# Sixty instructions change places within their engine's queue in a hybrid attention layer

## The chip, the cores and the metric

The kernel runs on one core of a Trainium2 chip. The core has five engines with a queue of instructions each: TensorE (PE, matrix products; its weight loads are listed apart as PEld), VectorE (DVE), ScalarE (ACT), GpSimd (POOL) and SyncE (SP), which in this kernel issues every DMA. [...] The metric is the time of one execution on the device in microseconds (us), lower is better. A profiled execution is a little different from the timed ones, so its own time is given beside its span.

## The reference

One layer of an encoder: a norm, one input projection, two kinds of attention side by side, an output projection and an embedding gate. It is computed for a prompt of 1024 tokens and a sample of 32 tokens that has caches of 512 positions.

```python
qa, ka, va, ga, qb, kb, vb, gb = split(rmsnorm(h, g_pre) @ w_in)   # 8 x 512 columns
oa = band_attention(qa, ka, va)       # 8 heads of 64, own 64-frame chunk and the 8 before, relative bias, softmax
ob = stick_breaking(qb, kb, vb)       # 8 heads of 64, strictly causal
# stick-breaking: w = exp(log_sigmoid(z) + sum over later keys of log_sigmoid(-z))
y  = concat([oa * silu(ga), ob * silu(gb)]) @ w_out
h  = h + rmsnorm(y, g_post)
h  = h + sigmoid(h @ w_ple_gate) * (p @ w_ple)
return h for prompt and sample, and the new keys and values of both
```

All of it is float32. D_MODEL is 1024, w_in is 1024 x 4096, and the keys and values that are returned are those of each of the 16 heads.

## The kernel before

**Tiling and stages.** The 1056 tokens are worked in three groups of 352 columns. Products are made in a reduced float32 form, and each operand is split into a high and a low part (names with h and l: `wh_`, `wl_`, `wTh`, `wTl`), so that most products are three matmuls. The attention goes in eight stages, one pair of heads each, in turn A (band) and B (stick-breaking): A0, B0, A1, B1 and so on to A3 and B3. In a stage the two heads' scores, weights and values are woven with the projection (`col_steps`) of a later pair's q, k or v. Names carry this: `wTlA31_1` is the low part of the turned weights of A, pair 3, head 1, second set; `wr_vB3_0` the first half of the raw weight columns of v for pair 3 of B. After the stages follow the gates (`mm_g...`), then the output projection and the embedding gate.

**What the stages move by DMA.** The steps that the change and the prediction speak of:

- `load_w` (line 689) loads raw weight columns `wr_...`, two halves of 256 KB. `ensure` (line 701) has them rounded on ACT or POOL (`wh_`) and the rest subtracted on POOL (`wl_`).
- `weights_t` (line 1107) turns the attention weights. A part goes through PE (`ptw`, then ACT `wTh`, DVE `wTl`). The rest goes over a DRAM scratch: a transposed tile `om` is stored to `swap...`, four loads bring it back into `wTl`, 32 partitions each, ACT rounds `wTl` to `wTh`, and POOL or DVE subtracts. Only then can the products with the values run.
- `values` (line 1156) makes these products (`PVA`, `PVB`), adds the halves of the result into `ot`, and stores it to `o_dr`. `one_dr` takes the sums of the rows of A; `ogg` and `oneg` read `o_dr` and `one_dr` back at the gates.
- `keys_out` (line 867) transposes the keys to `ktA` or `ktB`, issues four stores to the output in pieces of 32 columns (128 bytes), and one of the sample's keys to `ks_dr`. `values_out` (line 886) does this for the values (`vx`, `swap`, `stv`, `vt`).
- `sample_attention` (line 1194) loads caches (`Kcs`, `Vcs`), biases (`biass`) and the sample's values (`vns`).
- `sum_weights` (line 1558) adds up blocks of the two later weight matrices (`oB`, `gB`) and stores the sums to `sum_dro` and `sum_drg`. `pp` holds a part of the embedding input p.

**What sets the order.** No instruction is issued when its line is reached. A `Recorder` notes all of them with what they read and write. `Recorder.order` (line 480) puts them into one list: a planner with a cost of each instruction, a key by which the urgent one goes first, and eight lanes for the DMAs, since each DMA also waits until the eighth before it has landed. `Recorder.moved` (line 557) splits this list into the queues of PE, ACT, DVE, POOL and SP and goes through `MOVES` in turn: a tuple of an engine, a place and a distance takes the instruction out that is at this place of the engine's queue at that moment, and puts it back the distance further on (or ahead, when it is negative). Then it merges the queues into one list again in which every instruction comes after all that it depends on. `Recorder.emit` (line 597) issues that list, all of it from line 607, which is why every row of the profile has line L607 and the tiles' names tell the rows apart. Only the places in the queues matter on the chip. SP's queue has 812 DMAs, and an issue that has to wait holds back every one behind it.

Of the kernel before, what the change touches and what calls it, by code (L numbers as in the profile page):

```python
# [115 lines left out]
def f(ap):  # L116
# [3 lines left out]


MOVES = (
    ("SP", 5, -1), ("ACT", 4, -1),
)


# [2002 lines left out]
```

## Time and profile before

| | before |
|---|---|
| median of three runs | 780.15 us (777.79 to 785.06) |
| profiled execution, its own time | 776.75 us |
| profiled execution, span | 775.0 us |
| mean granted clock of TensorE | 0.996 |
| DMA, mean over the span | 220 GB/s, 187836 packets, 170.57 MB |
| packets under 512 bytes | 65569 |

The profile's page gives busy time by engine, the span in forty slices, and groups of instructions by line, engine and tile. Its rows of a timeline have the start, the duration, the engine, the line, the operation with the tile written and the tiles read, how many instructions the row takes together, and in brackets the idle time of the engine just before and what released it. SPq stands for an issue of a DMA by SP: its duration is how long SP was held by the issue, not how long the transfer took. In the chain of waits a row "DMA" goes from the issue to the landing.

The forty slices show PE busy through the whole span, with a granted clock at its top value, while the share of the DMA engines in use goes up and down:

```profile
PE   8999999999999999999999998999999999999997
PEclk9999999999999999999999999999999999999999
DMA  9727988558996468986669698899479857669743
```

### The profile page before, as it was taken

Reading aid. Unit: us, or ns where it says so; the run is one execution under the profiler, and the core shown is the slowest. Engines: PE = TensorE matmul, PEld = TensorE weight load, DVE = VectorE, ACT = ScalarE, POOL = GpSimd, SP = SyncE. Lnnn points to the kernel's source line nnn. Section 1 sums busy time; section 2 is a strip of 40 time slices with the busy share of each in tenths; the row PEclk is TensorE's granted clock in tenths of the full one; section 3 lists DMA queues with packets and bytes.
Section 4 is the critical chain, followed back from the end, with each engine's and each line's share of the span. In section 5 each row is a group of like instructions: output and inputs, shape, how many; then the busy total and the mean of one; then the engine's idle time right before and its main releaser. Section 6 shows DMA issues by size and latency. Waiting matters only on the chain.

```text
span 775.0 us, 14078 instructions
## 1 busy us (share of the span) xinstructions
PE 756.9 (98%) x4462; PEld 701.2 (90%) x4462; DVE 592.8 (76%) x1029; ACT 540.0 (70%) x1115; POOL 498.6 (64%) x531
## 2 busy tenths in 40 slices
PE   8999999999999999999999998999999999999997
PEld 7999989999999999999999898989998877888786
DVE  7718778886888878778797677787564687999965
ACT  6646977887777769797886577555447868777451
POOL 5733868993746569478994437877652539698533
PEclk9999999999999999999999999999999999999999
DMA  9727988558996468986669698899479857669743
GB/s 298 248 77 214 265 250 252 159 158 280 212 262 162 113 193 204 301 245 201 183 195 268 165 246 228 212 225 265 130 269 305 291 167 248 233 210 351 231 152 136
DMA packets 187836, 170.57 MB, mean 220 GB/s; under 512 B 65569, under 2 KB 149705, under 8 KB 186738
## 3 DMA queue, kind: packets, MB, share of 16 engines
q1 hardware_dynamic: 187762, 169.68, 75.0%
q8 instruction: 35, 0.57, 0.3%
q14 instruction: 39, 0.32, 0.2%
HBM read 108.34 MB, written 61.53 MB: 219 GB/s over the span
## 4 chain that ended last, share of the span: by engine, by line
PE 78%; DMA 8%; SPq 4%; DVE 3%; ACT 3%; issue 3%; POOL 1%; ACTq 0%; POOLq 0%; DVEq 0%
PE mm_gB L607 6%; PE mm_kB L607 6%; PE mm_kA L607 6%; PE mm_vA L607 5%; SPq L607 4%; PE mm_qB L607 4%; PE mm_qA L607 4%; PE PVB L607 3%; PE mm_vB L607 3%; PE SA L607 3%; PE PVA L607 3%; PE ple L607 3%; DMA wTl<-swapA 3%; PE SB L607 3%; PE o3P L607 3%
## 5 line engine op out<-in xcount | busy, mean ns | idle before, releaser
L607 POOL TENSOR_TENSOR be<-be,om 128x1024 f32<-128x1024 f32 (+8 forms) x66 | 84.7, 1290 | 39.6 <-DVE om L607 21.7
L607 DVE TENSOR_TENSOR_SCAN om<-om,SB 128x384 f32<-128x384 f32 (+5 forms) x96 | 92.0, 963 | 14.9 <-ACT be L607 5.9
L607 POOL TENSOR_TENSOR wTl<-wTl,wTh 128x1280 fp32r<-128x1280 f32 (+3 forms) x26 | 58.2, 2242 | 12.2 <-ACT wTh L607 10.7
L607 ACT ACTIVATE om<-SB 128x512 f32<-128x512 f32 (+5 forms) x96 | 45.3, 492 | 17.3 <-DVE SB L607 8.2
L607 ACT ACTIVATE be<-be,statA 128x640 f32<-128x640 f32 (+3 forms) x64 | 44.3, 694 | 15.9 <-DVE statA L607 15.7
L607 DVE STREAM_TRANSPOSE om<-be 128x640 f32<-128x640 f32 (+2 forms) x56 | 49.9, 893 | 4.8 <-POOL be L607 2.6
L607 ACT ACTIVATE be<-SB 128x384 f32<-128x384 f32 (+5 forms) x96 | 45.1, 495 | 10.0 <-DVE SB L607 5.7
L607 ACT CAST wTh<-wTl 128x1280 fp32r<-128x1280 f32 (+3 forms) x40 | 39.6, 1003 | 13.7 <-DMA wTl<-swapA 7.7
L607 DVE TENSOR_TENSOR wTl<-wTl,wTh 128x1280 fp32r<-128x1280 f32 (+3 forms) x14 | 28.5, 2035 | 12.6 <-ACT wTh L607 9.6
L607 DVE CUSTOM_DVE_ANT_0 be<-SA,biasA 128x320 f32<-128x320 f32 (+3 forms) x64 | 29.8, 478 | 7.2 <-PE SA L607 4.3
L607 PE MATMUL SB<-kdB,LB 128*128 128x512 f32 (+5 forms) x96 | 33.5, 353 | 0.7 <-DVE LB L607 0.4
L607 POOL TENSOR_TENSOR gB<-gB,gB 128x256 f32<-128x256 f32 x32 | 25.8, 824 | 10.9 <-DMA gB<-in_w_ple_gate_dram 10.9
L607 PE MATMUL SB<-kl,LB 128*128 128x512 f32 (+5 forms) x96 | 32.4, 346 | 0.0
L607 PE MATMUL SA<-kdA,LA 128*128 128x320 f32 (+2 forms) x96 | 30.4, 320 | 0.0
L607 PE MATMUL SA<-kl,LA 128*128 128x320 f32 (+2 forms) x96 | 30.0, 316 | 0.0
L607 DVE TENSOR_TENSOR SB<-SB,maskb 128x128 f32<-128x128 f32 x64 | 17.6, 291 | 12.9 <-PE SB L607 12.2
L607 DVE TENSOR_TENSOR wTl<-ptwB,wTh 128x512 fp32r<-128x512 f32 (+3 forms) x48 | 25.8, 545 | 2.1 <-ACT wTh L607 1.5
L607 ACT CAST wTh<-ptwB 128x512 fp32r<-128x512 f32 (+3 forms) x48 | 22.6, 480 | 6.2 <-PE ptwB L607 4.4
L607 POOL TENSOR_TENSOR oB<-oB,oB 128x256 f32<-128x256 f32 x32 | 24.0, 771 | 4.5 <-DMA oB<-in_w_out_dram 4.5
L607 PE MATMUL PVB<-wTl,v2B 128*128 128x256 f32 (+1 forms) x144 | 24.8, 294 | 0.5 <-POOL om L607 0.5
L607 POOL TENSOR_TENSOR kl<-stkB,kdB 64x1024 fp32r<-64x1024 f32 x8 | 19.2, 2405 | 9.0 <-issue 6.8
L607 PEld LDWEIGHTS PVB<-wTh,v2B 128*128 128x128 f32 x144 | 20.9, 189 | 3.3 <-ACT wTh L607 2.9
(700 smaller groups left out, 2665.6 us busy)
## 6 DMA issues: line engine op xcount, KB each, us to landing
swapA<-om SPq DMA_DIRECT2D x8, 1280.0 KB, 6.0
wTl<-swapA SPq DMA_DIRECT2D x32, 320.0 KB, 5.9
oB<-in_w_out_dram SPq DMA_DIRECT2D x16, 256.0 KB, 4.3
sum_dro<-oB SPq DMA_DIRECT2D x16, 256.0 KB, 3.9
gB<-in_w_ple_gate_dram SPq DMA_DIRECT2D x16, 256.0 KB, 4.5
sum_drg<-gB SPq DMA_DIRECT2D x16, 256.0 KB, 3.2
x<-in_x_prompt_dram SPq DMA_DIRECT2D x16, 256.0 KB, 4.2
h_dr<-h SPq DMA_DIRECT2D x8, 512.0 KB, 4.1
```

Of the source, the lines that this page charges most:

```text
L607: getattr(getattr(tc.nc, o.what[0]), o.what[1])(*args, **kw)
```

## The change

`MOVES` grows from two tuples to sixty-two. No instruction is added, removed or altered, no tile changes its size or number of buffers, and nothing else in the file is touched. Of the new tuples 42 are for SP, 9 for ACT, 5 for DVE and 2 each for PE and POOL. Since they are carried out one after the other and some undo a part of an earlier one, 144 DMAs, 33 instructions of ACT, 13 of DVE, 12 of PE and 9 of POOL stand at another place in the end. The tuples for SP lie in groups of neighbouring places: around 59 to 89, 134 to 148, 177, 197 to 208, 325 to 345, 371 to 376, 444, 455 to 477, 491 to 526, 534 to 550 and 566 to 594.

```diff
 MOVES = (
-    ("SP", 5, -1), ("ACT", 4, -1),
+    ("SP", 5, -1), ("ACT", 4, -1), ("SP", 462, 5), ("SP", 84, 5), ("SP", 494, 4), ("SP", 501, 1),
+    ("SP", 197, 5), ("SP", 71, 11), ("SP", 325, 16), ("SP", 136, 12), ("SP", 148, -14),
+    ("SP", 517, 9), ("SP", 526, -3), ("SP", 521, 5), ("SP", 59, -1), ("SP", 455, 3),
+    ("ACT", 282, 15), ("SP", 540, -5), ("SP", 537, -1), ("SP", 536, -2), ("SP", 339, 6),
+    ("SP", 201, 7), ("DVE", 281, -1), ("SP", 72, 13), ("ACT", 347, -1), ("SP", 491, 7),
+    ("SP", 460, 9), ("PE", 1607, 8), ("SP", 444, 1), ("DVE", 512, 1), ("SP", 456, 1),
+    ("ACT", 724, -1), ("SP", 470, 3), ("SP", 466, 4), ("DVE", 513, -2), ("ACT", 353, 2),
+    ("ACT", 669, -4), ("SP", 331, 3), ("SP", 460, 6), ("SP", 550, -1), ("SP", 543, 4),
+    ("SP", 376, -5), ("SP", 566, 2), ("SP", 592, 2), ("SP", 568, 5), ("DVE", 87, 6),
+    ("ACT", 725, 1), ("ACT", 626, 2), ("POOL", 313, 5), ("SP", 177, -1), ("SP", 468, 9),
+    ("DVE", 188, -1), ("POOL", 59, 2), ("SP", 541, -5), ("SP", 85, 2), ("PE", 3188, -2),
+    ("SP", 507, -5), ("ACT", 627, -1), ("SP", 546, -1), ("SP", 509, 9), ("SP", 522, -3),
+    ("ACT", 667, -3),
 )
```

In the terms of the tiles, the groups that the prediction speaks of do this in the end (places in SP's queue, before and after):

- 71 and 73 to 81 and 87: two stores of ktB0 go from ahead of the store of swapA01 to just before and among the loads of wTlA01. The load at 84 goes to 89, behind a store of sums (86) and one of o_dr0 (88).
- 325 to 340 and 340 to 345: the loads wr_qA3_1 and wr_vA3_0 go behind the loads of wTlA20 and the store of swapA21.
- 460 to 477, 461 to 466, 462 to 469: the store of vtA3 and two stores of ktB3 go behind the load wr_vB3_0 (465 to 462) and the load vnsA1 (467 to 464).
- 491 to 498 and 494 to 497: a store of o_dr3 and a load of wTlA31 go behind the other three loads of wTlA31 (495 to 497, now 493 to 495).
- 536 to 534 and 540, 541 to 537, 536: a load of pp and two loads of wTlB30 come forward; the load oggA2 goes from 535 to 538.

## The prediction

> **What bounds the kernel now.** I read the busy table first, then the table of waits of TensorE (PE), then its timeline around every wait, and last the queue of SyncE (SP), which issues all DMAs.
>
> ```profile
> PE 756.9 (98%) x4462; PEld 701.2 (90%) x4462; DVE 592.8 (76%) x1029; ACT 540.0 (70%) x1115; POOL 498.6 (64%) x531
> ```
>
> ```profile
> PE PVA L607 <- ACT wTh L607: 4.4, 4, 2.9
> PE PVB L607 <- ACT wTh L607: 2.3, 2, 1.7
> PE mm_vB L607 <- ACT wh_vB L607: 1.4, 2, 1.3
> PE idle L607 <- DVE newh L607: 1.3, 1, 1.3
> PE ple L607 <- ACT wph1True L607: 0.6, 1, 0.6
> PE mm_gA L607 <- ACT stvB L607: 0.5, 1, 0.5
> ...
> PE ptp L607 <- DMA pp<-in_p_prompt_dram: 0.4, 1, 0.4
> ...
> PE ptwB L607 <- DVE wTl L607: 0.2, 1, 0.2
> ```
>
> PE is the bound: 756.9 of 775.0 us busy. The thirteen rows of waits, of which the first and the last stand here, sum to 12.9 us (us in total, times, longest). Three of them (1.3, 0.6, 0.4) lie at the start, where nothing is moved, and the smaller PVB wait (2.3 less 1.7) has no move near it. So about 10.0 us is all that a new order can take from the waits. They lie here:
>
> ```profile
> 112.43 1.52 PE L607 MATMUL PVA<-wTh,v2A 128*128 128x512 f32 x8 [0.15 <-ACT wTh L607]
> 167.88 0.63 PE L607 MATMUL ptwB<-ident,be 128*128 128x128 f32 x4 [0.18 <-DVE wTl L607]
> 329.13 1.09 PE L607 MATMUL PVA<-wTh,v2A 128*128 128x512 f32 x4 [1.10 <-ACT wTh L607]
> 435.08 0.42 PE L607 MATMUL mm_vB<-hnh,wh_vB 128*128 128x352 f32 x1 [1.28 <-ACT wh_vB L607]
> 438.23 0.91 PE L607 MATMUL mm_vB<-hnh,wh_vB 128*128 128x352 f32 x4 [0.17 <-ACT wh_vB L607]
> 469.01 2.61 PE L607 MATMUL PVA<-wTh,v2A 128*128 128x512 f32 x8 [2.87 <-ACT wTh L607]
> 506.39 0.92 PE L607 MATMUL PVB<-wTh,v2B 128*128 128x256 f32 x6 [1.70 <-ACT wTh L607]
> ```
>
> The bracket is PE's idle time and its releaser. ACT is the name given, but it waits for a load each time (rows below), so these are waits on the DMA queue. There is one more loss:
>
> ```profile
> 466.00:468.90 2.90, 0.14 (x1) 0.00 (x0) 0.92 (x3) 2.37 (x3) 1.03 (x1) 1.00 1.01 411
> 468.90:472.40 3.50, 3.39 (x12) 3.20 (x13) 1.12 (x3) 3.05 (x8) 3.50 (x2) 0.51 0.73 166
> 503.00:506.40 3.40, 1.70 (x12) 1.41 (x10) 1.18 (x3) 1.54 (x4) 0.14 (x2) 1.00 1.09 256
> ```
>
> In the table by stretches (stretch, length, busy time of PE, its loads, DVE, ACT, POOL, then granted clock, DMA share, GB/s) the clock is 0.51 for the 3.5 us behind the 2.87-us gap: half of 3.4, so 1.7 us, is lost. The 1.70-us gap cost no clock.
>
> **The change part by part.** Nothing is added or removed. 60 moves leave 144 of SP's 812 issues at another place, 33 instructions of ACT, 13 of DVE, 12 of PE and 9 of POOL. SP's queue runs in order, so a store postponed behind a load brings the load forward, and a waiting issue holds all behind it. Going through the trace in time:
>
> *Stage of vB3 (moves at SP 444 to 477, DVE 512/513, POOL 313).*
>
> ```profile
> 421.58 8.26 SPq L607 DMA_DIRECT2D out_dram<-ktB  x4
> 429.95 1.67 SPq L607 DMA_DIRECT2D wr_vB<-in_w_in_dram  x1
> ```
>
> ```profile
> 434.41 0.62 ACT L607 CAST wh_vB<-wr_vB 128x512 fp32r<-128x512 f32 x1 [3.04 <-DMA wr_vB<-in_w_in_dram]
> ```
>
> Four stores of ktB hold SP for 8.26 us; behind them the load of wr_vB is issued, and its cast, 3.04 us idle, ends at 435.03, where PE waits. The change puts two of the four ktB stores and the vtA store behind this load. Two of four issues of 8.26 are about 4 us, three times the 1.28 + 0.17 us to be won, so even with half of it lost to queued transfers both waits go: −1.4 (between −1.0, if vnsA, also moved forward here, keeps ACT, and −1.45). Cover lost: the postponed stores have no reader in the kernel but the end. DVE, POOL and SP 444: results read much later, 0.
>
> *Stage of wTlA31 (SP 491 to 526, ACT 626/627).*
>
> ```profile
> 454.93 1.10 SPq L607 DMA_DIRECT2D o_dr<-otA  x2
> 456.71 1.83 SPq L607 DMA_DIRECT2D wTl<-swapA  x4
> ```
>
> ```profile
> 458.11 8.35 DMA wTl<-swapA
> ```
>
> ```profile
> 466.54 2.42 ACT L607 CAST wTh<-wTl 128x1280 fp32r<-128x1280 f32 x2 [3.62 <-DMA wTl<-swapA]
> ```
>
> One o_dr store (half of 1.10) goes behind the four loads; three loads go ahead by that, but the fourth goes behind one_dr, at the slot where the last load was. The last load takes 8.35 us from issue to landing and the cast needs all four, so the gain is between 0 and 0.55; I take −0.4, because the store's packets also leave the front. Of 2.87 us then 2.5 remain. ACT's two moves exchange activations that PE does not wait for: 0.
>
> The clock behind it: bounds 0 and −1.7. A gap of 2.5 lies between the 2.87 that lost the clock and the 1.70 that did not. I take −1.7: the slow stretch began exactly as the gap ended (468.9), and with some 2 us won ahead of it the gap ends 2.4 us earlier, so a 3.4-us stretch counted back from 468.9 would then hold over 2 us of work. This is the weakest term.
>
> [...]
>
> *Stage of wTlB30 (SP 534 to 550, ACT 667/669).*
>
> ```profile
> 487.89 6.33 DMA pp<-in_p_prompt_dram
> ...
> 501.55 3.91 DMA wTl<-swapB
> ```
>
> ```profile
> 494.28 2.88 SPq L607 DMA_DIRECT2D onegA<-one_dr  x4
> ```
>
> In the chain of waits the issue at 494.28 waits for the landing of pp (487.89 + 6.33 = 494.22), and from there SP issues back to back to the last wTl load at 501.55, which the 1.70-us gap waits for. The pp load goes forward by two slots of about 0.6, so it lands some 1.2 earlier, but two wTl loads now stand between it and the others. I take −0.6 of the 1.70 (0 if queued packets set the landing, −1.2 if the issue does).
>
> *Stage of wTlA20 (SP 325, 331, 339).*
>
> ```profile
> 308.30 0.75 SPq L607 DMA_DIRECT2D wr_qA<-in_w_in_dram  x1
> ```
>
> ```profile
> 318.44 5.12 DMA wTl<-swapA
> ```
>
> ```profile
> 342.12 0.62 ACT L607 CAST wh_qA<-wr_qA 128x512 fp32r<-128x512 f32 x1
> ```
>
> The wr_qA load of 0.75 goes behind the four wTl loads, whose last is issued at 318.44. Its reader comes at 342.12, so the postponement to about 323 is covered by 19 us. All issues behind 308.30 go ahead by up to 0.75: −0.7 of the 1.10 (0 to −1.1).
>
> *Stage of wTlA01 (SP 59, 71, 72, 84, 85, DVE 87, POOL 59).* This one goes the other way.
>
> ```profile
> 84.76 6.38 SPq L607 DMA_DIRECT2D out_dram<-ktB  x3
> ...
> 99.42 1.79 SPq L607 DMA_DIRECT2D wTl<-swapA  x4
> 101.25 0.43 SPq L607 DMA_DIRECT2D one_dr<-sumA  x1
> 101.78 1.14 SPq L607 DMA_DIRECT2D o_dr<-otA  x2
> ```
>
> ```profile
> L607 SPq DMA_DIRECT2D out_dram<-ktB x16: 321/868/4968, 82.6 to 429.3; - x16
> ```
>
> ```profile
> 100.78 8.07 DMA wTl<-swapA
> ```
>
> Two of three ktB stores leave the front of 84.76 and come down among the wTl loads; one of these loads goes behind one_dr, a ktB store and the first o_dr. It is issued at about 101.78 + 0.57 = 102.35, where the last load now goes out between 100.78 and 101.25: 1.1 to 1.6 later, less what the packets of ktB, gone from the front, had delayed. PE waits 0.15 for this cast already, so a delay is paid in full: +0.4 (−0.15 to +1.5). A ktB issue takes 321 to 4968 ns; the long end is a rival below. DVE and POOL moves: 0.
>
> *Small ones.* DVE 188 puts the wTl subtraction that PE waits for at 167.88 ahead of another:
>
> ```profile
> 166.66 0.74 DVE L607 TENSOR_TENSOR Kl0sA<-ksS,Kh0sA 128x32 fp32r<-128x32 f32 x1
> ```
>
> That is 0.74 against a wait of 0.18: −0.18. PE 1607 and ACT 347/353 (around 257 to 264) fill waits of 0.2 each: −0.16. SP 136/148 (net two places), 177, 197/201, 376, 566 to 592, ACT 282, 724/725, DVE 281, PE 3188 shift work whose readers come over 5 us later, or at SP 201 keep a wTl load in the slot of the last one: 0, ±0.3 together.
>
> *Sum:* −1.4 −0.4 −1.7 −0.6 −0.7 +0.4 −0.18 −0.16 = −4.75. The profiled execution took 776.75 (span 775.0), so it would take 772.0. It stands 3.4 below the median of the runs, 780.15; I put the same difference on the median: **775.4 us**.
>
> **The rivals.** *All of it goes:* if each stage's last load is brought forward by enough, the 10.0 us of waits and the 1.7 of clock go: 780.15 − 11.7 = 768.4. For it: a wait like 435.08 goes wholly. Against it: the last wTl load at 469.01 and 506.39 keeps nearly its place.
>
> *The clock stays halved:* the gap before 469.01 remains above the 1.70 that is known to be harmless; then −3.05 and 777.1. [...]
>
> *A ktB store stalls SP at 99 to 102 (slower):* one ktB store now stands in front of the last wTlA01 load. In the trace its issue took up to 4.97 us against 0.87 in the median, when queued transfers had to drain. If it does so here, the load is 4.97 − 0.87 = 4.1 later, and with the 1.5 above PE waits up to 5.6 at 112.43, and loses 1.7 of clock after it: +7.3 instead of +0.4, in all −4.75 + 6.9 = +2.2, so 782.3. It decides (slower than before) from a stall of about 2 us on if the clock falls, of 3.7 if not. Against it: only one store, not three or four, and the pile of short packets that came with them is parted.
>
> *It does nothing:* if the DMA engines and not SP's issues set the landings (in the stretch 466.00 to 468.90 the DMA share is 1.01, none free), the order inside a few us is of no account: 780.15.
>
> **How the numbers follow.** Forecast 0.42 (own range 773.5 to 777); all of it goes 0.2; clock stays 0.15; nothing 0.13; stall 0.1. About 1% (7.8 us) is what a measurement of this kernel can tell from no change, since its runs lie between 777.79 and 785.06. Faster by over 1% (below 772.3): the 0.2 of the first rival and 0.05 of the forecast's lower end, 0.25. Slower by over 1% (above 788): the stall with more of the same behind it, 0.05. Within: 0.7. The range goes from the first rival, 768.4, to just short of the stall, 781.7; 0.2 is left out.
>
> **What would show it.** Right: no wait at 435, about 0.4 at 329 and 1.1 at 506, 2.5 at 469 with the clock at 1.0 behind it, about 0.5 at 112. Wrong: a ktB issue of over 3 us between wTl loads near 100; a wait of 2.8 at 469 still; a new wait of PE on a weight cast whose load was postponed (wr_qA, wr_vA, KcsB1).

## The result and the profile after

The changed kernel takes 771.43 us in the median of three runs (770.59 to 774.78), where the one before took 780.15: a ratio of 0.9899 with a 95% interval of 0.9859 to 0.9938. Run again in another set it was 771.46 against 779.77, ratio 0.9900 (0.9871 to 0.9930). The profiled execution took 770.59 us, span 768.8, so 6.2 us less than the profiled one of before.

The page's busy table and the waits of TensorE (us in total, times, longest) in the changed kernel:

```profile
PE 754.5 (98%) x4462; PEld 699.8 (91%) x4462; DVE 588.2 (77%) x1029; ACT 540.3 (70%) x1115; POOL 502.8 (65%) x531
```

```profile
PE PVA L619 <- ACT wTh L619: 2.9, 3, 1.4
PE PVB L619 <- ACT wTh L619: 2.1, 2, 1.3
PE idle L619 <- DVE newh L619: 1.3, 1, 1.3
PE ptp L619 <- DMA pp<-in_p_prompt_dram: 1.2, 1, 1.2
...
PE mm_gA L619 <- ACT stvB L619: 0.2, 1, 0.2
```

The waits on wh_vB have gone, the longest wait on wTh has fallen from 2.9 to 1.4, and the wait for pp at the start, where nothing was moved, is 0.8 longer by chance. PE's timeline shows the places that the prediction named; these seven lines are from seven stretches of it:

```profile
112.42 1.51 PE L619 MATMUL PVA<-wTh,v2A 128*128 128x512 f32 x8 [0.86 <-ACT wTh L619]
...
327.02 0.64 PE L619 MATMUL PVA<-wTh,v2A 128*128 128x512 f32 x2
...
345.75 1.51 PE L619 MATMUL PVA<-wTh,v2A 128*128 128x512 f32 x8 [0.64 <-ACT wTh L619]
...
382.73 0.86 PE L619 MATMUL PVB<-wTh,v2B 128*128 128x512 f32 x4 [1.27 <-ACT wTh L619]
...
465.26 1.52 PE L619 MATMUL PVA<-wTh,v2A 128*128 128x512 f32 x8 [1.42 <-ACT wTh L619]
...
482.05 1.16 PE L619 MATMUL PVB<-wTh,v2B 128*128 128x256 f32 x8 [0.85 <-ACT wTh L619]
...
500.30 0.83 PE L619 MATMUL PVB<-wTh,v2B 128*128 128x256 f32 x6
```

The rows at 327.02 and 500.30 are the matmuls that were at 329.13 and 506.39: no idle time stands in front of them. At 465.26 (469.01 before) the wait is halved, at 112 it is longer. Three waits are new or longer: 346, 383 and 482. In the stretches around the gap the clock stays at its top:

```profile
463.85:465.30 1.45, 0.04 (x1) 0.04 (x1) 0.77 (x3) 1.45 (x3) 1.18 (x1) 1.00 1.01 400
465.30:468.70 3.40, 3.40 (x21) 3.30 (x22) 2.23 (x5) 3.40 (x9) 3.40 (x2) 1.00 1.05 256
```

At the stage of vB3 the load wr_vB stands behind two stores of ktB instead of four. In SP's queue it is issued at 424.12 (before: 429.95), and in ScalarE's timeline its cast waits 0.17 us instead of 3.04:

```profile
420.56 2.57 SPq L619 DMA_DIRECT2D out_dram<-ktB  x2
424.12 3.76 SPq L619 DMA_DIRECT2D wr_vB<-in_w_in_dram  x1
```

```profile
430.69 0.62 ACT L619 CAST wh_vB<-wr_vB 128x512 fp32r<-128x512 f32 x1 [0.17 <-DMA wr_vB<-in_w_in_dram]
```

### The profile page after: what moved, and what is told of

Its sections match the earlier page's. It is cut to its first block, busy times and chain, and to the rows that moved or that the text cites. A ratio compares the mean times of both kernels' runs of the same rounds, so it can differ in the third digit from the quotient of the medians.

```text
span 768.8 us, 14082 instructions
## 1 busy us (share of the span) xinstructions
PE 754.5 (98%) x4462; PEld 699.8 (91%) x4462; DVE 588.2 (77%) x1029; ACT 540.3 (70%) x1115; POOL 502.8 (65%) x531
## 4 chain that ended last, share of the span: by engine, by line
PE 80%; DMA 9%; ACT 3%; SPq 3%; POOL 2%; DVE 2%; issue 1%; ACTq 0%; POOLq 0%; DVEq 0%
PE mm_gB L619 6%; PE mm_vA L619 6%; PE mm_kB L619 5%; PE mm_kA L619 5%; PE mm_qA L619 5%; PE PVB L619 4%; PE mm_vB L619 4%; DMA wTl<-swapA 4%; PE SA L619 3%; PE mm_qB L619 3%; PE SB L619 3%; PE ple L619 3%; PE PVA L619 3%; PE mm_gA L619 3%; PE o3P L619 3%; PE g1P L619 3%
## 5 line engine op out<-in xcount | busy, mean ns | idle before, releaser
L619 DVE TENSOR_TENSOR wTl<-wTl,wTh 128x1280 fp32r<-128x1280 f32 (+3 forms) x14 | 26.5, 1892 | 10.0 <-ACT wTh L619 9.0
L619 POOL TENSOR_TENSOR sggB<-sggB,oggB 128x352 f32<-128x352 f32 x12 | 13.6, 1137 | 16.3 <-DVE sggB L619 11.1
```

What stands on the lines that cost most here:

```text
L619: getattr(getattr(tc.nc, o.what[0]), o.what[1])(*args, **kw)
```

## The experiments

Twelve runs were made: ten new kernels, one of them twice, and the changed kernel once more. Each move touches only the places between its start and its end, so the moves of one group of places can be left out or made alone. The diffs show `MOVES` without the two tuples of before. Places are named by the time at which the matmul stands in the profile of before. A few keep the time of the profile in which they were first seen: 346 and 482 (347.15 and 486.16 in the profile of before), 466 (the same place as 469), 496 (499.06) and 205 (201.43). The kernel before was run again beside each set of four, and the sets ran on different chips (its medians there: 778.42, 779.77, 778.00), so kernels of different sets are compared by their ratios.

### The change again

```diff
 MOVES = (
     ("SP", 5, -1), ("ACT", 4, -1), ("SP", 462, 5), ("SP", 84, 5), ("SP", 494, 4), ("SP", 501, 1),
...
```

> The changed kernel once more, beside the kernel before on this chip. Theory (what one profiled execution shows of a wait is one draw; the order decides which waits can occur): the median lies 5 to 8 us under that of before; the waits at 329, 435, 438 and 506 are 0 to 0.3 again, those at 112, 346, 383, 466 and 482 differ by up to 1 us from the first profile. Rival (the first three runs were low by chance): under 3 us faster.

771.46 us (six runs, 769.72 to 777.23) against 779.77. The waits at 329, 435, 438 and 506 are gone again; 112 is 0.66, 346 is 0.36, 383 is 0.54, 466 is 1.68, 482 is 0.64. So two draws of the same kernel differ by up to 0.73 us at one place. From here on one profile's wait is read as one draw, and the table behind the experiments has all fourteen.

### One group at a time

Around the loads of wTlA31 (nine of SP, two of ACT):

```diff
+    ("SP", 494, 4), ("SP", 501, 1), ("SP", 517, 9), ("SP", 526, -3), ("SP", 521, 5),
+    ("SP", 491, 7), ("ACT", 626, 2), ("SP", 507, -5), ("ACT", 627, -1), ("SP", 509, 9),
+    ("SP", 522, -3),
```

> Only the moves around the loads of wTlA31 and KcsB1 (SP 491 to 526, ACT 626/627). Theory (the order there is itself worth the gain): the wait of 2.87 at 469 falls to about 1.5, the clock behind it stays at 1.0, some 2.7 us faster than before in the profiled execution. Rival (only 0.4 is its own, the rest came from work further ahead): a wait of about 2.5 with the clock halved behind it, under 1 us faster.

777.18 us, ratio 0.9985 (0.9966 to 1.0004). The wait at 469 is 2.35, as the rival had it, but the clock behind it stays whole, as the theory had it; and a wait of 1.19 at 482 is new. What is won at 469 is given back at 482, and since the interval holds 1, a gain in the time is not shown.

Around the load of wr_vB3:

```diff
+    ("SP", 462, 5), ("SP", 455, 3), ("SP", 460, 9), ("SP", 444, 1), ("DVE", 512, 1),
+    ("SP", 456, 1), ("SP", 470, 3), ("SP", 466, 4), ("DVE", 513, -2), ("SP", 460, 6),
+    ("POOL", 313, 5), ("SP", 468, 9),
```

> Only the moves around the loads of wr_vB3 (SP 444 to 477, DVE 512/513, POOL 313). Theory of independent waits: 1.28 and 0.17 at 435 and 438 gone, the wait at 469 unchanged at 2.9, clock halved behind it, 1.7 us faster than before. First rival (the loads at 469 land when the DMA queue lets them, and PE just arrives earlier): the wait at 469 grows to about 4.3, no gain. Second rival (fewer transfers queued later): the wait at 469 falls under 2.4.

776.46 us, ratio 0.9978 (0.9957 to 0.9999), about 1.7 us. Both waits are gone, and one of 0.21 is new at the matmul right behind, 435.40. The wait at 469 is 2.40 with half a clock behind it. It has not grown to 4.3, so the first rival falls. 2.40 is at the edge of the second rival (under 2.4), but the kernels without moves at that place have 2.08 to 2.87 there, so it is not clearly smaller. The gain is kept, as the theory of independent waits has it.

Around the loads of wTlA01:

```diff
+    ("SP", 84, 5), ("SP", 71, 11), ("SP", 59, -1), ("SP", 72, 13), ("DVE", 87, 6),
+    ("POOL", 59, 2), ("SP", 85, 2),
```

> Only the moves around the loads of wTlA01 (SP 59 to 85, DVE 87, POOL 59). Theory by the last three profiles (without these moves the wait at 112 was 0.15, 1.36 and 1.00, with them 0.86, 0.82, 0.85): the wait at 112 is 0.8 to 0.9 and the sum of the waits at 98, 102 and 112 is 0.8 to 0.9 too, against 0.9 to 2.0 without; time 0 to 1 us under before. Rival (the load that goes last costs what was forecast): the sum is 1.3 or more, no gain.

778.35 us, ratio 0.9989 (0.9966 to 1.0012). The sum of the three waits is 0, lower than either expectation; the profiled execution had other waits instead (0.98 at 206, 1.97 at 383, 1.78 at 435) and two stretches of half clock. No loss, and no gain that can be told from none.

Around the loads of wTlB30:

```diff
+    ("SP", 540, -5), ("SP", 537, -1), ("SP", 536, -2), ("ACT", 669, -4), ("SP", 550, -1),
+    ("SP", 543, 4), ("SP", 541, -5), ("SP", 546, -1), ("ACT", 667, -3),
```

> Only the moves around the loads of wTlB30 (SP 534 to 550, ACT 667/669). Theory (these alone take the wait of 1.70 at 506, which stood at 1.70, 0.66, 1.33 and 1.29 without them and at 0 in all runs with them): the wait is under 0.3, no new wait within 10 us of it, time 1 to 1.8 us under before. Rival (the wait only goes if work ahead is early too): the wait stays above 0.6.

776.45 us, ratio 0.9975 (0.9957 to 0.9993), about 1.9 us. The wait at 506 is gone:

```profile
507.06 0.82 PE L609 MATMUL PVB<-wTh,v2B 128*128 128x256 f32 x6
```

This is the matmul that waited 1.70; no bracket stands behind it. The theory holds: these moves take the wait by themselves.

### All but one group: the loads of wTlA20

```diff
-    ("SP", 325, 16), ("SP", 339, 6), ("SP", 331, 3),
```

> All moves but the three around the loads of wTlA20 (SP 325, 331, 339). Theory (the 1.4 us won at 329 are paid back at 346 and 383, since the loads wr_qA3_1 and wr_vA3_0 that went behind now stand in front of the loads of wTlA21): the wait of 1.1 at 329 is there again, those of 0.64 and 1.27 at 346 and 383 are back to 0 and 0.6 or less, time within 0.5 us of the changed kernel. Rival (the gain is real, and the later waits have other causes): the wait at 329 is there and those at 346 and 383 stay, so 1.4 us slower.

773.37 us (four runs), ratio 0.9931 (0.9911 to 0.9951), where the change has 0.9900: 0.31%, or 2.4 us, though the two intervals overlap. The wait at 329 is back with 1.28, and those at 346 and 383 stay with 0.71 and 1.19: the rival is right. The postponed loads wr_qA3_1 and wr_vA3_0 do not cause the later waits.

### SP alone, and the other engines alone

```diff
-    ("ACT", 282, 15), ("DVE", 281, -1), ("ACT", 347, -1), ("PE", 1607, 8),
...
-    ("POOL", 59, 2), ("PE", 3188, -2), ("ACT", 627, -1), ("ACT", 667, -3),
```

> The 42 moves of SP alone, the 18 on PE, ACT, DVE and POOL undone. Theory (the DMA order carries the gain): time within 1.5 us of the changed kernel's 771.4; the waits of 0.18 at 167.9 and 0.24 at 261 come back, no other. Rival (a good part comes from the other engines' moves): a time of 775 or more, and besides these two a wait of the kernel before stands again at 469 or 506.

> The 42 moves of SP alone once more. Theory (the first such run's 776.0 had a chance part: a wait of 2.54 at 205, where a VectorE subtraction took 6.2 us beside a run of POOL adds, and half a clock after it): no wait over 1 us at 205, median 772 to 774.5. Rival (the moves of the other engines keep that wait away): the wait is there again, median 775.5 or more.

776.04 and 774.73 us, ratios 0.9965 (0.9939 to 0.9992) and 0.9963 (0.9934 to 0.9991). In the first run the time is the rival's, but not for the rival's reason: at 506 there is no wait, and the one at 469 (2.13) lies where it lies in other kernels with the same moves. What costs the time is new. Both profiled executions have a wait of 2.5 us at 205 that no other of the fourteen has. In the second one it is this (VectorE, then GpSimd, then TensorE):

```profile
195.63 6.20 DVE L615 TENSOR_TENSOR Vl0sA<-be,Vh0sA 128x512 fp32r<-128x512 f32 x1
```

```profile
195.29 2.52 POOL L615 TENSOR_TENSOR wl_vB<-wr_vB,wh_vB 128x512 fp32r<-128x512 f32 x2
197.77 3.50 POOL L615 TENSOR_TENSOR oB<-oB,oB 128x256 f32<-128x256 f32 x5
```

```profile
203.42 0.66 PE L615 MATMUL ptwA<-ident,be 128*128 128x128 f32 x4 [2.53 <-DVE wlsA L615]
```

VectorE's subtraction takes 6.20 us and ends 0.56 behind the last of seven POOL instructions that follow one another without a pause (197.77 + 3.50 = 201.27). In the changed kernel the same seven stand there, and the same subtraction takes 1.48:

```profile
195.94 1.48 DVE L619 TENSOR_TENSOR Vl0sA<-be,Vh0sA 128x512 fp32r<-128x512 f32 x1
```

```profile
195.58 3.00 POOL L619 TENSOR_TENSOR wl_vB<-wr_vB,wh_vB 128x512 fp32r<-128x512 f32 x2
198.53 3.71 POOL L619 TENSOR_TENSOR oB<-oB,oB 128x256 f32<-128x256 f32 x5
```

So the rival of the second run is right that the wait is there again, though the median of 774.73 lies between the two expectations. The 18 others alone:

```diff
+    ("ACT", 282, 15), ("DVE", 281, -1), ("ACT", 347, -1), ("PE", 1607, 8),
...
+    ("POOL", 59, 2), ("PE", 3188, -2), ("ACT", 627, -1), ("ACT", 667, -3),
```

> The 18 moves on PE, ACT, DVE and POOL alone, no move of SP. Theory (they are worth the small waits they touch): the waits of 0.18 at 168, 0.24 at 261 and 0.48 at 461 go or fall under 0.2, all others stay in the spread of the kernels without SP's moves, and the time is 0.5 to 1.2 us under before. Rival (the 4 us between SP's moves alone, 776.0, and the whole change, 771.5, are theirs): 2.5 us or more under before.

778.58 us, ratio 1.0003 (0.9985 to 1.0020). The small waits go as expected (168 and 261 to 0, 461 from 0.48 to 0.20), but the time falls neither by the 0.5 to 1.2 us of the theory nor by the rival's 2.5. By themselves these moves are worth nothing that can be measured; beside SP's moves the time is some 5 us lower with them than without (0.9900 against 0.9964), of which the wait at 205 with the half clock behind it makes 2.5 + 1.7 (in the second profile a granted clock of 0.50 from 204.07 to 207.48). Two of two profiles without them had this wait, and none of the three with them in which the same seven POOL instructions follow one another (both of the change, and the one with the otA store put back). That is few enough for chance, and which of the 18 does it was not tried: this stays open.

### Mending what the change left

The wait at 482. One store added to the change's list:

```diff
     ("ACT", 667, -3),
+    ("SP", 526, -4),
```

> The change, and the store of otA31_1_0 to o_dr3 put back ahead of its neighbour (SP 526 to 522). Theory (the new wait of 0.85 at 482 comes from this store: ACT idled 1.45 us until it had landed, because the copy into otA needs its buffer, and the cast of wTh stands behind that copy): ACT does not wait there any more and the wait at 482 is under 0.2, time 0.5 to 1 us less than the changed kernel. Rival (the loads of wTlB30_2, late since KcsB1 went ahead, set it): the wait stays above 0.6.

ScalarE in the changed kernel, and with the store put back:

```profile
480.15 0.37 ACT L619 COPY otA<-PVA 64x256 f32<-64x256 f32 x1 [1.45 <-DMA o_dr<-otA]
480.54 0.62 ACT L619 CAST wh_gA<-wr_gA 128x512 fp32r<-128x512 f32 x1
481.07 0.93 ACT L619 CAST wTh<-wTl 128x896 fp32r<-128x896 f32 x1
```

```profile
480.28 0.36 ACT L619 COPY otA<-PVA 64x256 f32<-64x256 f32 x1
480.67 0.62 ACT L619 CAST wh_gA<-wr_gA 128x512 fp32r<-128x512 f32 x1
481.20 0.94 ACT L619 CAST wTh<-wTl 128x896 fp32r<-128x896 f32 x1
```

The wait of 1.45 is gone in front of the copy, and PE has none at 482. So the cause was the postponed store: `ot` has three buffers, and the copy could not have its own until the store had landed. The time is 771.63 us (ratio 0.9894), no less than the change's 771.46 in the same set. The profiled execution lost 2.26 us at 469 and half a clock behind it; and a gain of 0.5 to 1 us, as expected, is too small for these runs to show, since the intervals of the two ratios are 0.45% and 0.59% wide (3.5 and 4.6 us).

Four places:

```diff
     ("ACT", 667, -3),
+    ("SP", 526, -4), ("SP", 490, 7), ("SP", 487, 9), ("SP", 405, -3), ("SP", 89, -3),
```

> The change with four more places mended: the otA store as in the run beside this; the loads wr_gA2_0 and wr_gA2_1, which are read 25 us later, behind the loads of wTlA31; the store swapB21_6 ahead of two weight loads and a ks_dr store; the last load of wTlA01 ahead of one_dr0, ktB0 and o_dr0 stores. Theory (each of these waits is the time the DMA queue needs for what stands ahead, so 512 KB taken from the front is worth about 2 us of landing): the waits at 112, 383, 466 and 482 (0.86, 1.27, 1.42, 0.85) fall to under 0.3 each, and the median is 2.5 to 4 us under the changed kernel's. Rival (the landings follow from earlier transfers anyway, or the waits come up at the next place): two or more of the waits stay within 0.4 of what they were, median within 1.5 us.

772.18 us, ratio 0.9895 (0.9872 to 0.9917): no gain over the change. Of the four waits those at 112, 383 and 482 are gone, as the theory had it; the one at 466 fell to 0.92 and not under 0.3. That 512 KB are worth about 2 us was the author's estimate; at the mean of 220 GB/s in the profile of before they make 2.4. The second half of the rival came true, a new wait further on, with half a clock behind it:

```profile
496.38 0.50 PE L620 MATMUL SB<-kdB,LB 128*128 128x512 f32 x1 [2.14 <-DVE om L620]
```

Three of the four, without the loads of wr_gA2:

```diff
     ("ACT", 667, -3),
+    ("SP", 526, -4), ("SP", 405, -3), ("SP", 89, -3),
```

> The change with three more places mended: the otA store (SP 526 to 522), the store swapB21_6 ahead of two weight loads (405 to 402), the last load of wTlA01 ahead of three stores (89 to 86); the loads of wr_gA2 stay where the change has them. Theory (in the run with four places the load wr_gA2 behind wTlA31 made SP's full queue late up to 502 and so made the wait of 2.14 at 496): no wait over 0.5 at 496, those at 112, 383 and 482 under 0.3, the one at 466 about 1.4 to 2.3; median 0.5 to 2.5 us under the changed kernel's 771.5. Rival (waits that are taken away come up at the next place): median within 0.5 us of it or above.

769.16 us (six runs, 767.48 to 772.35), ratio 0.9883 (0.9858 to 0.9909). The lowest of all here, 0.17% under the change's 0.9900; the two intervals overlap, so that it beats the change is likely and not shown. The waits went as the theory had it: those at 112, 383 and 482 are gone, 0.27 is left at 496, and 2.29 stands at 469, with half a clock. At 506 a wait of 1.13 is back. So the moves of wr_gA2 won about 1.4 us at 469 and cost about 1.9 at 496, one profile each.

### The waits of all profiled executions

TensorE's idle time (us) in front of the matmul of the given place, named as above; 0 is under 0.1. "98" is the sum of the places 98, 102 and 112, "435" that of 435 and 438. Other places (the start, 206, 388, 431, 496) have waits of up to 2.1 in single profiles. "Half" is the length of half clock between the first and the last matmuls.

```
kernel            98    205    329    346    383    435    469    482    506    half
before           0.92   0      1.10   0      0.58   1.45   2.87   0      1.70   3.4
wTlA31 only      2.03   0      1.36   0      1.26   1.14   2.35   1.19   0.66   0
vB3 only         1.00   0      0.76   0.17   1.81   0      2.40   0      1.33   3.4
wTlA01 only      0      0      0.83   0      1.97   1.78   2.25   0      1.29   6.8
others only      0.77   0      1.22   0.20   2.41   1.31   2.08   0      1.17   3.4
wTlB30 only      0.74   0      1.23   0.94   1.13   1.47   2.85   0      0      6.8
SP only          0.82   2.54   0      0      1.54   0      2.13   0.67   0      3.4
SP only again    0.47   2.53   0.27   0      1.05   0      1.63   1.02   0      3.4
without wTlA20   0.85   0      1.28   0.71   1.19   0      2.03   0.64   0      3.4
change           0.86   0      0      0.64   1.27   0      1.42   0.85   0      0
change again     0.66   0      0      0.36   0.54   0      1.68   0.64   0      0
otA store back   0      0      0.20   0      1.07   0      2.26   0      0      3.4
four more        0      0      0.23   0      0      0.45   0.92   0      0      3.4
three more       0      0      0.27   0      0      0      2.29   0      1.13   3.4
```

## Why the prediction was right, and where it was wrong

The changed kernel is faster, as forecast, and its time lies in the range, between the forecast's 775.4 and the first rival's 768.4. It is nearer to the rival (3.0 us) than to the forecast (4.0). The gain is about double the forecast's: 8.7 us in the medians against 4.75 (the terms as printed add up to 4.74). The median lies below the forecast's own range (773.5 to 777), and just over the 1% up to which the text called it no change; that had been given 0.7, and faster by more than 1% only 0.25. The rival that comes nearest in time is not what happened either: not all waits went, 1.42 and 1.68 stayed at 469 in the change's two profiles, and new ones came at 346 and 482.

*The stage of vB3 (−1.4).* Right in mechanism and nearly in size: 1.45 goes in eight of nine profiles with these moves (0.45 is left in one), and alone they are worth 1.7 us in the medians. What it left out: 0.2 comes back at 435.40 in all nine, and in none of the five without, so that some 1.2 is left at this place.

*The stage of wTlA31 (−0.4).* The wait at 469 is 2.49 on average in the five kernels without these moves and 1.97 in the eight with them that leave wr_gA2 where it was: −0.5, near what was forecast, though these kernels differ in other moves too, and in the change itself the wait is 1.42 and 1.68. Wrong is what the prediction left out. It put the other moves there at nothing. The store of o_dr3 that goes from 522 to 526 is among them, and it holds a buffer of otA: in all six profiles that have it there, ScalarE's copy waits 1.2 to 2.3 us until it has landed, and TensorE 0.83 at 482 on average. So the group as a whole is worth little. That "ACT's two moves exchange activations that PE does not wait for" is wrong too: the wait at 461 (0.48) is 0.2 in every kernel with them, a gain of 0.3 at that place.

*The clock (−1.7).* Right for the first profile, by luck, and not for the reason given. The forecast had a gap of 2.5 us shifted to where the clock would not fall. That the clock hangs on the work in a 3.4-us stretch was the author's assumption: the profile of before shows, between its first and last matmuls, one piece at 0.50, 3.41 us long, behind the gap of 2.87. In the change's profiles the gap is 1.42 and 1.68: the first lies whole within one of the stretches of the last section (462.83 to 466.24), so no shift saved the clock there, the gap was short. A shift can't be forecast from one profile either: the stretches of the last section are laid from the first moment of full clock, which came anywhere from 4.2 to 10.2 us in the fourteen executions (4.69 in the profile of before, 5.49 in that of the change). And the same order with one store moved lost the clock again, with a gap of 2.26. As an average, though, the term holds. The granted clock of every run is on record: its mean is 0.9983 over nine runs of the change and 0.9960 over the 71 of the kernel before that ran beside the experiments, which makes 1.3 and 3.1 us of lost clock, 1.8 less. With the moves of wTlA31 alone it is 0.9980 in ten runs, against 0.9959 beside them.

*The stage of wTlB30 (−0.6).* Undersized. Without the moves the wait is 1.23 on average over five profiles, with them 0 in eight of nine (1.13 in one). "−1.2 if the issue does" was the right size, but not by the issue alone. The last of these loads is issued 4.5 us before TensorE is free for it on average in the five and 5.2 in the nine, so 0.7 earlier, and it takes 4.8 us from issue to landing in the five and 3.8 in the nine, so 1.0 less. In the profile of before the late issue stands out (3.1 us ahead, 3.9 to land), in the other four the long landing.

*The stage of wTlA20 (−0.7).* 1.11 on average in the seven profiles without, 0.14 in the seven with: about −1.0, and leaving it out costs 2.4 us in the medians, with half a clock in its profile that the change's two do not have. The cover of the postponed loads held.

*The stage of wTlA01 (+0.4).* The sign was wrong. The step that failed reads: "PE waits 0.15 for this cast already, so a delay is paid in full". The 0.15 was one draw; the sum of the waits there is 1.09 on average in five profiles without the moves and 0.52 in the seven with the change's order of these DMAs. At 112 alone it is 0.65 and 0.52, no rise; the rest of the difference is at 98 and 102. The load does go out later, as worked out: at 102.05 in the changed kernel, while the last load of the kernel before goes out at 100.78. But the delay was not paid: the cast that needs it starts at 108.93 in the changed kernel and at 108.95 in that of before, 6.9 and 8.2 us behind the issue. With this group alone the load goes out at 103.61 and the cast starts at 109.10. So the later load was there as early; that the packets of ktB which had gone from the front made room for it is the likely reason, not tried by itself. The store that was feared between the loads held SP for 0.42 us, with a DMA share of 0.91 from 99 to 103; the issue of 4.97 us in the kernel before stood in a stretch with 1.08 (190 to 203), and that queued transfers held it was the author's reading. The third rival, the slow one, falls with this.

*DVE 188 and the moves around 257 to 264 (−0.18, −0.16).* The waits of 0.18 and 0.24 are 0 in every kernel with the moves; the one of 0.47 at 264 stays.

*From the profile to the median.* "I put the same difference on the median" was another error. The profile of before was better than its kernel's usual run, by 3.4 us, and the profiled one of the change by 0.84 (771.43 − 770.59). At 383, for instance, 0.58 stood in the profile of before and 1.0 to 2.4 in ten of the eleven others in which swapB21_6 kept its place. This makes 2.6 us of the 4.0 between gain and forecast.

*Do the parts make up the whole?* Groups made alone give 0.15% (wTlA31), 0.22%, 0.11% and 0.25%; the group of wTlA20, from leaving it out, 0.31%; the other engines 0. That is 1.04%, and the whole is 1.0%; but each part is known to about 0.2% only, so the agreement is loose. SP alone, though, gave 0.36%, since its profiles have the wait at 205.

## What to carry to other kernels

With an engine at 98% and several hundred DMAs on one queue, what was won by order here lay in single waits of 1 to 3 us; find each in the timeline, follow it to the load, and look at what stands ahead of that load in the queue that its consumer needs later. A store that is postponed is not free because nobody reads its data: the one of otA held its buffer, and the next writer, ScalarE's copy, waited 1.45 us. Take several profiles before a wait of under 1 us is given a number, and try moves together as well as alone: the 18 of the other engines are worth nothing by themselves here, and the time with SP's moves is some 5 us lower beside them, for a reason that stays open.

## What the runs showed of the hardware

**Half clock came for 3.41 us at a time, behind stretches of that length with little work, and not always behind the longer gap.** In the profile of before the granted clock is 0.50 from 468.91 to 472.32, and nowhere else between the first and the last matmuls. Laying stretches of 3.41 us end to end from the first moment of full clock, in each of the fourteen executions, every stretch with 2.03 us or more of idle TensorE was followed by 3.41 us at half clock (eleven of them, 2.03 to 2.77); of thirteen with 1.4 to 1.9 two were (1.47 and 1.78), and none below. What sets these two apart from the other eleven, this count does not show. The end of the half clock falls on the same grid. Two executions show it side by side, without the loads of wTlA20 first, and with the moves of wTlA31 alone behind it:

```profile
466.84:470.25 3.41, 1.38 (x8) 0.99 (x7) 1.26 (x3) 3.36 (x5) 2.02 (x1) 1.00 1.05 397
470.25:473.66 3.41, 3.41 (x15) 3.41 (x14) 2.73 (x5) 3.25 (x8) 3.41 (x3) 0.50 0.93 211
```

```profile
468.38:471.79 3.41, 1.55 (x10) 1.26 (x8) 2.30 (x4) 1.98 (x2) 0.64 (x1) 1.00 1.03 396
471.79:475.20 3.41, 2.92 (x18) 2.82 (x19) 1.71 (x5) 3.41 (x9) 3.41 (x2) 1.00 0.94 231
```

The shorter gap, 2.03 us, lay in one stretch, and the next one ran at 0.50, which cost 1.7. The longer, 2.35, was cut by the grid into 1.86 and 0.49 (3.41 less the busy time), and the clock stayed at 1.00.

**The same VectorE subtraction took 1.48, 3.4 or 6.2 us beside a run of POOL instructions.** These are its times in the fourteen executions: 1.48 in the changed kernel, 3.43 in the one before, 6.20 in the one shown above. In the eight executions with over 3 us it ended 0.55 us behind the last of several POOL instructions that followed one another without a pause, three of them in six executions, seven in two. What held it, no trace shows. In seven of the eight it had started 0.338 to 0.347 us after the first POOL instruction, in all six with 1.48 0.359 to 0.365 after; the eighth, at 0.368, took 3.42. What decides between these times was not settled.
